# A hybrid DeltaNet / RWKV-7 layer on one core: output passes that sum in PSUM by an identity product, five input buffers, and loads placed with a lead time

## The chip, the core and the metric

The kernel runs on one core of one Trainium2 chip. A core has TensorE (PE; its weight loads are shown as PEld), VectorE (DVE), ScalarE (ACT), GpSimd (POOL) and SyncE (SP), which here issues every DMA. Each engine executes its own instructions strictly in the order in which the program lists them; semaphores hold an instruction back until its inputs are there. The metric is the device time of one launch in microseconds (us); lower is better.

## What is computed

A backbone layer with a batch of one, 512 latent tokens, a 256-token context prefix and 2048 channels. Cut to what matters:

```python
h  = rmsnorm(x)   * (1 + scale) + shift          # and hc for the context
u  = h @ w_in                                    # (512, 2048) @ (2048, 8 kinds x 8 slots x 128 and some small columns)
ya = gdn_mixer(uc, u)                            # gated DeltaNet, 8 heads of 128, both directions
yb = rwkv_mixer(uc, u)                           # RWKV-7, 16 heads of 64, both directions
x  = x + gate[:, None] * (concat([ya, yb]) @ w_out)   # the output projection, contraction over 2048 channels
return rmsnorm(x, final_norm_g)
```

Everything is fp32. A large product is made of three matmuls in the chip's fp32r format: each operand is split into a high and a low part, and high x high, high x low and low x high are summed.

## The kernel before, in words

**Slots.** The heads are worked off in eight slots: slot i holds DeltaNet head i and RWKV heads 2i and 2i+1. After a front (conditioning, norms, small projections) the context phase runs through the eight slots, then the latent phase through the eight slots again. In each slot `mixer` does: preparation (`prep_g`, `prep_r`, `prep_d`, `blocks`), `send` (a triangular matrix Z goes to DRAM as DA), `solve` (30 elimination steps on DVE, each one product solT and one update solNL; the result goes to DRAM as DD), `levels` (loads lt and Z from DD, and 96 small matmuls in the latent phase), `chain` (8 dependent steps over the chunks of 64 tokens) and `outp` (norms and gates; y is stored to the DRAM tensor yd). The chains of two slots alternate between two sets of buffers ("lanes"), so slot i+2 can only be prepared when slot i has left its lane.

**Big products.** The projections of the latent tokens (`proj`) fill PE beside the mixers until the third latent slot. The output projection follows in four *passes* (`out_pass`): pass 0 takes the y of slots 0 and 1, pass 1 slots 2 and 3, pass 2 slots 4 and 5, pass 3 slot 6; slot 7 is done at the end by `out_last`. Passes 0 to 2 are made of 16 output tiles with 12 matmuls of 128x512 each, pass 3 of 16 tiles with 6. In the trace a pass's PSUM tile is accl, its weights are wh and wl (from wr), its input is yh and yl. The running sum stays in DRAM (`rt_d`, in the trace rtd): for each tile ACT takes the PSUM result times the gate into xt, POOL adds xr (the sum so far, loaded from rtd; x itself in pass 0), and SP stores xt to rtd. Pass 3 adds rtd into the SBUF tensor rt by one DVE instruction.

**What sets the order.** The kernel is first recorded, then a list scheduler (`Rec.schedule`) plans a start for each instruction from a table of costs, and the instructions are written out in the planned order of each engine. Three of its rules matter here. An edge between instructions of different engines has a latency from `LAT`; between two of the same engine from `OWN`, and where `OWN` has no entry, the second counts as free to start as soon as the first has *started*. SP has no entry, so the load that follows a store of the same DRAM data is planned right behind it. Matmuls of jobs and passes have a `fill` flag: they are taken where PE has nothing else, or has been too idle lately. And where PE would be idle too long, the scheduler puts in *warm* matmuls (wm<-zero, 128 columns of zeros) that do nothing but keep PE active. The plan is only an order: on the chip every instruction starts when its engine reaches it and its semaphores are there.

Of the kernel before, what the change touches and what calls it, by code (L numbers as in the profile page):

```python
# [148 lines left out]
OWN = {"V": 120, "A": 148, "G": 107}  # L149
# [118 lines left out]
class Op:  # L268
    __slots__ = ("eng", "fn", "args", "kw", "npred", "succ", "ready", "dur", "tiles", "need", "prio", "idx", "src",
                 "end", "ps", "bytes", "key", "hold", "rows", "passes", "sync", "pos", "load", "fill", "bun", "cells", "cls", "lock")  # L270
# [10 lines left out]
class Rec:  # L281
    hook = None

    def __init__(self, tc, cfg):
        import concourse.bacc as bacc
        self.tc, self.nc, self.cfg = tc, tc.nc, cfg
        self.scratch = bacc.Bacc("TRN2", target_bir_lowering=False, num_devices=1)
        self.protos, self.ops, self.tiles, self.lastpool = {}, [], [], None
        self.lookidx = 0
        self.psum_last, self.shift, self.fill, self.bun, self.nbun = {}, 0, 0, None, 0  # L290
        self.engs = {"V": self.nc.vector, "A": self.nc.scalar, "G": self.nc.gpsimd, "T": self.nc.tensor, "S": self.nc.sync}
# [12 lines left out]
    def new(self, eng, fn, args, kw):  # L304
        o = Op()
        o.eng, o.fn, o.args, o.kw = eng, fn, args, kw
        o.npred, o.succ, o.ready, o.tiles, o.need, o.end, o.bytes = 0, [], 0.0, [], [], None, 0
        o.sync, o.load, o.pos, o.fill = [], 0, -1, self.fill if eng == "T" else 0
        o.idx = len(self.ops)
        o.key = o.idx + self.shift  # L310
        o.bun = self.bun if eng == "T" else None
        if o.bun:
            o.bun.ops.append(o)
        o.src = Rec.hook() if Rec.hook else None
        self.ops.append(o)
        return o
# [35 lines left out]
    def record(self, eng, fn, args, kw):  # L352
# [41 lines left out]
        for a, sync in preds.items():  # L394
            if a.eng == eng:
                lat = OWN.get(eng, -1) if sync else -1
            else:
                lat = LAT.get(a.eng + eng, 0) if sync else 0
            self.edge(a, o, lat)
# [841 lines left out]
class Kernel:  # L1241
# [51 lines left out]
    def setup(self):  # L1293
# [3 lines left out]
        self.hl = self.pool("hl", side="right")  # L1297
        self.hc = self.pool("hc", side="right")
# [60 lines left out]
    def front(self):  # L1359
# [59 lines left out]
        for kt in range(KT):  # L1419
# [12 lines left out]
            ar = fp.tile([P, 256], F32, tag="ar", bufs=2, name=self.nm("ar"))  # L1432
# [40 lines left out]
        self.ul = self.pool("ul")  # L1473
# [104 lines left out]
    def bcast_rows(self, dst, col, nj, ones, pool, psum):  # L1578
        for g in range(0, nj, 4):
            m = min(4, nj - g)  # L1580
            ps = psum(g // 4)
            for j in range(m):
                dg = pool.tile([P, P], F32, tag="dg", bufs=2, name=self.nm("dg"))
# [17 lines left out]
    def proj(self, kind, i, ctx, lat, part=None):  # L1601
# [19 lines left out]
        if lat:  # L1621
            t = self.ul.tile([P, SEQ], F32, tag="ul", bufs=2, name=self.nm(kind))
# [25 lines left out]
    def u_load(self, kind, i):  # L1648
        tag = "uz" if kind[1] == "z" else "u"
        t = self.u[(kind, i, 1)] = self.mp.tile([P, SEQ], F32, tag=tag, bufs=(3, 1)[tag == "uz"], name=self.nm(kind))  # L1650
# [88 lines left out]
    def main(self):  # L1739
# [27 lines left out]
        for i in range(NSLOT):  # L1767
# [5 lines left out]
            if i == n0:  # L1773
                self.hl.release()
# [25 lines left out]
    def passes(self, i):  # L1800
        for p in self.cfg.get("passes", {"3": [0], "5": [1], "7": [2]}).get(str(i), []):
            self.rec.shift = self.cfg.get("osh", 1000)
            self.rec.fill = self.cfg.get("ofill", 9000)
            self.out_pass(p)
            self.rec.shift = self.rec.fill = 0
# [4 lines left out]
    def y_load(self, src, eng=None):  # L1810
        self.yh, self.yl = self.y_tiles()
        for q, j in enumerate(src):
            y = self.yl[:, q].bitcast(F32)
            self.S.dma_start(y, self.y_d[j])
            self.y_split(q, y, eng)
# [5 lines left out]
    def out_pass(self, p):  # L1821
# [5 lines left out]
        for i in range(KT):  # L1827
# [4 lines left out]
            else:  # L1832
                o = 2 * (i % 2)
                if o == 0:
                    hi, lo = self.split(self.I["wout"][24 + 8 * p + i // 2].rearrange("p (k m) -> p k m", m=P), eng)
            for k in range(n):
                for m, (w, hx) in enumerate(((hi, yh), (hi, yl), (lo, yh))):
                    self.mm(ps, w[:, o + k], hx[:, k], k == 0 and m == 0, k == n - 1 and m == 2)
            g = self.dvo["gt"][:, i:i + 1]
            if p == 3:  # L1840
                r = self.rt[:, i]
                self.S.dma_start(r, self.rt_d[:, i])
                self.stt(r, ps, g, r, ALU.mult, ALU.add)
                continue
            x, r = (self.xp.tile([P, SEQ], F32, tag=t, bufs=2, name=self.nm(t)) for t in ("xr", "xt"))
            self.S.dma_start(x, self.rt_d[:, i] if p else self.I["xt"][:, i, 0:SEQ])
            self.act(r, ps, AF.Copy, scale=g)
            self.tt(r, r, x, ALU.add, self.G)
# [60 lines left out]
    def close(self):  # L1909
# [4 lines left out]
        self.ul.release()  # L1914
# [27 lines left out]
```

## Time and profile before

| | us |
|---|---|
| median of 3 runs | 2160.66 (2158.78 to 2163.45) |
| the profiled execution | 2166.2 |
| its span in the trace | 2164.4 |
| PE busy | 1966.3 (91%) |
| DVE busy | 1475.2 (68%) |
| ACT busy | 815.9 (38%) |
| POOL busy | 640.2 (30%) |

PE's busy time contains 1846 warm matmuls. It is therefore no measure of how much PE has to do; the rows below tell the warm matmuls and the passes apart. PE names in the trace go by buffer: wm, pss and br are PSUM tiles that the mixers use, accl and accc those of the big products; "wm<-zero" alone is a warm matmul.

### The profile page before, as it was taken

The numbers are of one execution on the slowest core, as the hardware profiler recorded it, in microseconds if no ns is written. First come the engines' busy times: TensorE is split into PE (matmuls) and PEld (weight loads), VectorE is DVE, ScalarE is ACT, GpSimd is POOL, SyncE is SP. The second block draws the span as 40 slices with busy tenths as digits, with TensorE's granted clock in tenths as the row PEclk, the third lists the DMA queues.
The fourth block names the chain that finished last, engine by engine and source line by source line (L and its number), as shares of the span: only waits on it lengthen the run. The fifth ranks groups of instructions, "written<-read, shape, count | busy, mean of one in ns | idle before, by whom it ended". The sixth has DMA issues, their size and how long they took to land.

```text
span 2164.4 us, 44432 instructions
## 1 busy us (share of the span) xinstructions
PE 1966.3 (91%) x16999; PEld 1542.0 (71%) x17000; DVE 1475.2 (68%) x3397; ACT 815.9 (38%) x2127; POOL 640.2 (30%) x799
## 2 busy tenths in 40 slices
PE   7999999999999999999999999978887897889877
PEld 5678887777877778776777777756665666667666
DVE  6436578675867769574765865786868577767747
ACT  4443333333242433324434434436424452435235
POOL 0003404213140421101212202235823564246226
PEclk8999999999999999999999999999979899899998
DMA  8964433333333333344541542544631544044702
GB/s 305 358 221 109 114 92 95 94 89 88 95 98 90 103 101 88 84 114 124 143 133 47 157 128 67 177 140 143 202 87 44 150 154 136 24 123 123 229 12 97
DMA packets 230517, 269.33 MB, mean 124 GB/s; under 512 B 117280, under 2 KB 130080, under 8 KB 226208
## 3 DMA queue, kind: packets, MB, share of 16 engines
q1 hardware_dynamic: 230304, 266.49, 41.8%
q8 instruction: 133, 2.18, 0.4%
q14 instruction: 80, 0.66, 0.1%
HBM read 210.50 MB, written 55.89 MB: 123 GB/s over the span
## 4 chain that ended last, share of the span: by engine, by line
PE 51%; DVE 22%; DMA 12%; issue 5%; SPq 5%; ACT 3%; POOL 3%; DVEq 0%; ACTq 0%; POOLq 0%
PE accl L705 23%; PE wm L705 8%; PE pss L705 7%; PE br L705 7%; PE accc L705 6%; DVE solNL L705 6%; SPq L705 5%; DVE solT L705 4%; DMA DD<-solNL 3%; DVE Gk L705 3%; DVE wl L705 2%; DMA DA<-Z 1%; DVE t L705 1%; DMA solNL<-DA 1%; DMA yl<-yd 1%
## 5 line engine op out<-in xcount | busy, mean ns | idle before, releaser
L705 ACT ACTIVATE wh<-wr 128x512 fp32r<-128x512 f32 x312 | 196.1, 629 | 375.5 <-PE accc L705 144.3
L705 PE MATMUL accl<-hhi,wl 128*128 128x512 f32 x768 | 317.1, 413 | 10.9 <-DVE wl L705 10.9
L705 PE MATMUL accl<-hhi,wh 128*128 128x512 f32 x768 | 314.1, 409 | 1.8 <-issue 1.8
L705 PE MATMUL accl<-hlo,wh 128*128 128x512 f32 x768 | 312.7, 407 | 0.0
L705 DVE TENSOR_TENSOR wl<-wr,wh 128x512 fp32r<-128x512 f32 x264 | 187.6, 713 | 106.9 <-ACT wh L705 102.5
L705 PE MATMUL accl<-yh,wh 128*128 128x512 f32 x480 | 199.3, 418 | 22.0 <-ACT yh L705 13.8
L705 PE MATMUL accl<-yl,wh 128*128 128x512 f32 x480 | 198.7, 414 | 0.1
L705 PE MATMUL accl<-yh,wl 128*128 128x512 f32 x480 | 197.1, 412 | 1.5 <-DVE wl L705 0.9
L705 PEld LDWEIGHTS accl<-hhi,wl 128*128 128x128 f32 x768 | 146.9, 191 | 50.9 <-DVE wl L705 13.3
L705 DVE TENSOR_TENSOR solNL<-solNL,solT 48x30 f32<-48x30 f32 (+29 forms) x480 | 175.2, 365 | 10.3
L705 DVE TENSOR_TENSOR solT<-solNL 48x30 f32<-48x30 f32 (+29 forms) x480 | 170.6, 355 | 9.0
L705 POOL TENSOR_TENSOR SRd<-Sbd,Dd 64x128 f32<-64x128 f32 x160 | 71.1, 444 | 354.2 <-DVE Sbd L705 348.1
L705 PE MATMUL wm<-zero 128*128 128x128 bf16 x1846 | 146.2, 232 | 30.3 <-DVE SG L705 15.0
L705 PEld LDWEIGHTS accl<-hhi,wh 128*128 128x128 f32 x768 | 146.9, 191 | 20.6 <-issue 4.3
L705 PEld LDWEIGHTS accl<-hlo,wh 128*128 128x128 f32 x768 | 147.0, 191 | 20.2 <-issue 3.2
L705 PEld LDWEIGHTS <-zero 128*128 128x128 bf16 x1864 | 124.4, 105 | 51.7 <-issue 46.6
L705 PE MATMUL accc<-clo,wh 128*128 128x256 f32 x512 | 149.9, 293 | 0.0
L705 PE MATMUL accc<-chi,wh 128*128 128x256 f32 x512 | 147.6, 288 | 0.0
L705 PE MATMUL accc<-chi,wl 128*128 128x256 f32 x512 | 145.9, 285 | 0.0
L705 PEld LDWEIGHTS accl<-yh,wh 128*128 128x128 f32 x480 | 90.9, 191 | 43.2 <-ACT yh L705 15.0
L705 PEld LDWEIGHTS accc<-clo,wh 128*128 128x128 f32 x512 | 97.3, 190 | 24.1 <-issue 0.9
L705 PEld LDWEIGHTS accc<-chi,wh 128*128 128x128 f32 x512 | 97.3, 190 | 21.5 <-issue 0.7
(312 smaller groups left out, 4207.8 us busy)
## 6 DMA issues: line engine op xcount, KB each, us to landing
wr<-win SPq DMA_DIRECT2D x256, 256.0 KB, 3.2
wa<-wada SPq DMA_DIRECT2D x32, 1024.0 KB, 6.0
ud<-Gk SPq DMA_DIRECT2D x72, 256.0 KB, 2.6
gw<-wada SPq DMA_DIRECT2D x64, 256.0 KB, 3.5
wr<-wout SPq DMA_DIRECT2D x64, 256.0 KB, 2.9
Rk<-ud SPq DMA_DIRECT2D x48, 256.0 KB, 3.2
rtd<-xt SPq DMA_DIRECT2D x48, 256.0 KB, 2.2
xr<-rtd SPq DMA_DIRECT2D x32, 256.0 KB, 3.0
```

The costliest lines, as they stand in the source:

```text
L705: r = getattr(self.engs[o.eng], o.fn)(*args, **kw)
```

## The change

Five edits, none of which alters what the kernel computes.

1. **The sum over passes.** Passes 0 to 2 store the bare PSUM result to rtd (no gate, no POOL add). Passes 1 to 3 load the sum so far and let PE add it: an fp32 product of the identity with the loaded tile opens the accumulation of each output tile. Pass 3 ends with the one DVE instruction that multiplies by the gate and adds x, which is now loaded into rt from the input.
2. **Five buffers** instead of three for the loaded inputs u of the latent phase (Rk, Gk, Rr, Gv, Gq, Rv). Room comes from `ul`, which now is released in the middle of the latent phase; the second part of two-part projections takes its buffer from xp instead (in the trace such tiles, and the pass's x, are called Rr).
3. **Single buffers in the front** for ar and dg.
4. **Lead times.** A DMA recorded with `dsl` set counts as landing 2500 ns later in the plan (loads of the passes) or 6000 ns later (the passes' y).
5. **SP's own dependency** gets an entry in `OWN`: a DMA that needs an earlier DMA is planned 1500 ns after that one's landing instead of right behind its issue.

```diff
-OWN = {"V": 120, "A": 148, "G": 107}
+OWN = {"V": 120, "A": 148, "G": 107, "S": 1500}
...
                 lat = LAT.get(a.eng + eng, 0) if sync else 0
+                lat += a.dsl * sync
...
-            ar = fp.tile([P, 256], F32, tag="ar", bufs=2, name=self.nm("ar"))
+            ar = fp.tile([P, 256], F32, tag="ar", bufs=1, name=self.nm("ar"))
...
-                dg = pool.tile([P, P], F32, tag="dg", bufs=2, name=self.nm("dg"))
+                dg = pool.tile([P, P], F32, tag="dg", bufs=1 + (pool.name == "fin"), name=self.nm("dg"))
...
-        t = self.u[(kind, i, 1)] = self.mp.tile([P, SEQ], F32, tag=tag, bufs=(3, 1)[tag == "uz"], name=self.nm(kind))
+        t = self.u[(kind, i, 1)] = self.mp.tile([P, SEQ], F32, tag=tag, bufs=(5, 1)[tag == "uz"], name=self.nm(kind))
...
-            t = self.ul.tile([P, SEQ], F32, tag="ul", bufs=2, name=self.nm(kind))
+            pool, tag = (self.xp, "xr") if part == 1 else (self.ul, "ul")
+            t = pool.tile([P, SEQ], F32, tag=tag, bufs=2, name=self.nm(kind))
...
             if i == n0:
+                self.ul.release()
...
+            self.rec.dsl = self.cfg.get("odsl", 2500)
             self.out_pass(p)
+            self.rec.dsl = 0
...
+            d, self.rec.dsl = self.rec.dsl, self.cfg.get("ydsl", 6000)
             self.S.dma_start(y, self.y_d[j])
+            self.rec.dsl = d
...
+            if p:
+                x = self.xp.tile([P, SEQ], F32, tag="xr", bufs=2, name=self.nm("xr"))
+                self.S.dma_start(x, self.rt_d[:, i])
+                self.mm(ps, self.cs("ident"), x, True, False)
...
             if p == 3:
                 r = self.rt[:, i]
-                self.S.dma_start(r, self.rt_d[:, i])
+                self.S.dma_start(r, self.I["xt"][:, i, 0:SEQ])
                 self.stt(r, ps, g, r, ALU.mult, ALU.add)
                 continue
-            x, r = (self.xp.tile([P, SEQ], F32, tag=t, bufs=2, name=self.nm(t)) for t in ("xr", "xt"))
-            self.S.dma_start(x, self.rt_d[:, i] if p else self.I["xt"][:, i, 0:SEQ])
-            self.act(r, ps, AF.Copy, scale=g)
-            self.tt(r, r, x, ALU.add, self.G)
+            r = self.xp.tile([P, SEQ], F32, tag="xt", bufs=2, name=self.nm("xt"))
+            self.act(r, ps, AF.Copy)
             self.S.dma_start(self.rt_d[:, i], r)
```

Since the edits change the plan's inputs, the scheduler orders every engine anew. Over the whole program the instruction counts that differ are few: 48 POOL additions go, 48 identity products (accl<-Rr,cst 128x512) come, and the warm matmuls fall from 1846 to 1349. Two places show what moved.

**PE in the chain of the last slot** (slot 7; the products with SG, Sbd and SV open a step, those with Xs and VO follow in it). Before, the gaps between the chain's matmuls hold only warm ones:

```order
L705 MATMUL wm_0_124<-zero_0_65 128x128
L705 MATMUL wm_0_124<-SG_1_9315,KQ_0_12642 128x128 x2
L705 MATMUL pss_0_125<-Sbd_1426,KR_2_12647 128x128
L705 MATMUL pss_0_125<-Sbd_1426,KR_3_12648 128x128
L705 MATMUL pss_0_125<-SV_0_12649,Z_0_12641 64x64 x4
L705 MATMUL accc_0_134<-vn_0_9322,Z_0_12641 64x128 x2
L705 LDWEIGHTS zero_0_65
L705 MATMUL wm_0_124<-zero_0_65 128x128
L705 MATMUL pss_0_125<-Xs_0_9318,Z_0_12641 64x64 x4
L705 MATMUL wm_0_124<-VO_0_12636,Z_0_12641 64x128 x2
```

After, at the same place of a step of the same chain:

```order
L707 MATMUL accl_1_145<-yh_0_77,wl_2_1441 128x512
L707 MATMUL accl_0_144<-Rr_0_12489,cst_60 128x512
L707 MATMUL accl_0_144<-yh_0_77,wh_2_1438 128x512
L707 MATMUL wm_0_129<-SG_1_9339,KQ_0_12503 128x128 x2
L707 MATMUL pss_0_130<-Sbd_1429,KR_2_12508 128x128
L707 MATMUL pss_0_130<-Sbd_1429,KR_3_12509 128x128
L707 MATMUL pss_0_130<-SV_0_12510,Z_0_12502 64x64 x4
L707 MATMUL accc_0_139<-vn_0_9346,Z_0_12502 64x128 x2
L707 MATMUL accl_0_144<-yl_0_78,wh_2_1438 128x512
L707 MATMUL accl_0_144<-yh_0_77,wl_2_1441 128x512
L707 MATMUL pss_0_130<-Xs_0_9342,Z_0_12502 64x64 x4
L707 MATMUL wm_0_129<-VO_0_12497,Z_0_12502 64x128 x2
```

Pass 2 and pass 3 reach into the last slot's chain and beyond: behind the last slot's levels stand 131 pass matmuls and 18 identity products where none stood, and 144 warm matmuls where 324 stood.

**SP between a solve's result and the loads that need it**, latent slot 4. Before, the first load from DD stands directly behind the store:

```order
L705 DMA DD_0_119<-solNL_1424 96x2x1024
L705 DMA lt_0_9312<-DD_0_119 32x12x32
L705 DMA yd_111<-ot_1_9326 128x512
L705 DMA Gz_0_9292<-ud_110 128x512
L705 DMA Z_0_9337<-DD_0_119 32x12x32 x2
```

After, other transfers stand in between, among them a store of the pass's result (rtd<-xt), which waits for ACT, and loads of the sum so far (Rr<-rtd), which wait until PE has used their buffer:

```order
L707 DMA DD_0_124<-solNL_1427 96x2x1024
L707 DMA rtd_117<-xt_1_12492 128x512
L707 DMA Rr_1_12490<-rtd_117 128x512
L707 DMA wr_2_1435<-wout 128x512
L707 DMA Rk_0_9311<-ud_115 128x512
L707 DMA rtd_117<-xt_0_12491 128x512
L707 DMA Rr_0_12489<-rtd_117 128x512
L707 DMA lt_0_9336<-DD_0_124 32x12x32
```

In the program before, no DMA stands between store and first load at any of the 16 solves; after, one to eight do at each of them.

## Rows read from the trace of the kernel before

**Rows 1.** Stages of the latent phase by window, each from one slot's levels to the next.

```profile
core 0: us, PE busy (x) PEld busy (x) DVE busy (x) ACT busy (x) POOL busy (x), PEclk, DMA share, GB/s
...
1456.91:1591.32 134.41, 116.03 (x1175) 87.36 (x1174) 95.67 (x194) 58.81 (x159) 82.94 (x86) 0.95 0.52 158
1591.32:1683.61 92.29, 72.34 (x973) 56.81 (x972) 67.24 (x181) 35.17 (x114) 27.18 (x44) 0.88 0.24 66
1683.61:1823.84 140.23, 121.37 (x1264) 93.04 (x1262) 99.74 (x205) 58.77 (x162) 81.84 (x88) 0.93 0.49 145
1823.84:1918.68 94.84, 73.06 (x972) 56.98 (x971) 67.37 (x181) 35.24 (x114) 27.03 (x44) 0.87 0.23 65
1918.68:2044.85 126.17, 117.08 (x1039) 87.11 (x1037) 92.66 (x192) 50.55 (x122) 61.19 (x68) 0.95 0.59 178
2044.85:2164.39 119.54, 88.86 (x1145) 77.43 (x1144) 65.03 (x146) 49.45 (x131) 46.25 (x57) 0.88 0.18 56
```

**Rows 2.** The same windows, PE instructions on yh alone (two of each pass's three matmuls).

```profile
core 0: us, PE busy (x), PEclk, DMA share, GB/s
...
1591.32:1683.61 92.29, 2.77 (x8) 0.88 0.24 66
1683.61:1823.84 140.23, 45.02 (x120) 0.93 0.49 145
...
1918.68:2044.85 126.17, 64.19 (x180) 0.95 0.59 178
```

**Rows 3.** Two of the windows, PE instructions on zero (warm) alone.

```profile
1591.32:1683.61 92.29, 18.91 (x220) 0.88 0.24 66
1683.61:1823.84 140.23, 21.90 (x307) 0.93 0.49 145
```

**Rows 4.** Chain of waits: start us, length us, what; a run of 39 accl.

```profile
1994.49 9.11 PE accl L705 x39
```

**Rows 5.** Timeline of PE: start us, length us, instructions; warm, and fp32 of 512 columns.

```profile
1077.81 1.02 PE L705 MATMUL br<-t,cst 128*128 128x512 f32 x2
1078.67 0.60 PE L705 MATMUL br<-cst,t 128*128 128x128 f32 x4
...
2113.14 3.73 PE L705 MATMUL wm<-zero 128*128 128x128 bf16 x33
2116.63 0.56 PE L705 MATMUL accl<-yh,fh 128*128 128x256 f32 x1
```

**Rows 6.** Waits of PE: us in total, times, longest us.

```profile
PE wm L705 <- DMA lt<-DD: 29.0, 26, 2.6
...
PE accl L705 <- ACT yh L705: 14.6, 9, 3.2
...
PE accl L705 <- DVE wl L705: 11.8, 8, 3.2
```

**Rows 7.** Waits of SP's queue.

```profile
SPq L705 <- POOL xt L705: 80.7, 35, 6.7
...
SPq L705 <- DMA DD<-solNL: 60.0, 16, 4.7
```

**Rows 8.** Tile xt: instructions, duration ns min/median/max.

```profile
L705 POOL TENSOR_TENSOR xt<-xt,xr x48: 1261/1288/1751, 1482.9 to 2015.8; 128x512 f32<-128x512 f32 x48
```

**Rows 9.** Timeline of DVE and POOL in slot 5's solve.

```profile
1790.49 1.42 POOL L705 TENSOR_TENSOR xt<-xt,xr 128x512 f32<-128x512 f32 x1
1790.72 1.34 DVE L705 TENSOR_TENSOR KR<-t,t 128x126 f32<-128x126 f32 x1
1791.88 1.30 POOL L705 TENSOR_TENSOR wl<-wr,wh 128x512 fp32r<-128x512 f32 x1
1791.98 1.46 DVE L705 TENSOR_TENSOR solNL<-solNL,solT 96x240 f32<-96x240 f32 x1
1793.37 0.27 DVE L705 TENSOR_TENSOR KR<-t,t 128x126 f32<-128x126 f32 x1
1793.57 0.39 DVE L705 TENSOR_TENSOR solT<-solNL 96x238 f32<-96x238 f32 x1
```

**Rows 10.** Chain of waits in the front, the dg products.

```profile
32.76 2.13 PE br L705 x8
36.42 0.64 PE br L705 x4
```

**Rows 11.** Tile rt, DVE instructions, duration ns min/median/max.

```profile
L705 DVE SCALAR_TENSOR_TENSOR rt<-accl,dv,rt x32: 466/610/751, 2023.0 to 2144.9; 128x512 f32<-128x512 f32 x16, 128x256 f32<-128x256 f32 x16
```

More of the change, by code (lines that the diff above doesn't have):

```diff
@@ L269 @@
     __slots__ = ("eng", "fn", "args", "kw", "npred", "succ", "ready", "dur", "tiles", "need", "prio", "idx", "src",
-                 "end", "ps", "bytes", "key", "hold", "rows", "passes", "sync", "pos", "load", "fill", "bun", "cells", "cls", "lock")
+                 "end", "ps", "bytes", "key", "hold", "rows", "passes", "sync", "pos", "load", "fill", "bun", "cells", "cls", "lock", "dsl")
     def clone(self):
@@ L290, in __init__ @@
         self.psum_last, self.shift, self.fill, self.bun, self.nbun = {}, 0, 0, None, 0
+        self.dsl = 0
         self.engs = {"V": self.nc.vector, "A": self.nc.scalar, "G": self.nc.gpsimd, "T": self.nc.tensor, "S": self.nc.sync}
@@ L308, in new @@
         o.sync, o.load, o.pos, o.fill = [], 0, -1, self.fill if eng == "T" else 0
-        o.idx = len(self.ops)
+        o.idx, o.dsl = len(self.ops), self.dsl if eng == "S" else 0
         o.key = o.idx + self.shift
@@ L1297, in setup @@
         self.hl = self.pool("hl", side="right")
+        self.ul = self.pool("ul", side="right")
         self.hc = self.pool("hc", side="right")
@@ L1472, in front @@
         self.wp = self.pool("wp")
-        self.ul = self.pool("ul")
         self.upA = self.pool("upA")
@@ L1835, in out_pass @@
                     hi, lo = self.split(self.I["wout"][24 + 8 * p + i // 2].rearrange("p (k m) -> p k m", m=P), eng)
+            if p:
+                x = self.xp.tile([P, SEQ], F32, tag="xr", bufs=2, name=self.nm("xr"))
+                self.S.dma_start(x, self.rt_d[:, i])
+                self.mm(ps, self.cs("ident"), x, True, False)
             for k in range(n):
                 for m, (w, hx) in enumerate(((hi, yh), (hi, yl), (lo, yh))):
-                    self.mm(ps, w[:, o + k], hx[:, k], k == 0 and m == 0, k == n - 1 and m == 2)
+                    self.mm(ps, w[:, o + k], hx[:, k], not p and k == 0 and m == 0, k == n - 1 and m == 2)
             g = self.dvo["gt"][:, i:i + 1]
@@ L1913, in close @@
         self.mp.release()
-        self.ul.release()
         self.wp.release()
```

## The prediction

> **What bounds the kernel now.** I read the stages first, because the page's 91% for PE mixes three things. Up to the third latent slot PE works off the projections and is full. From there on the kernel goes by slots, and their stages alternate: 134.4, 92.3, 140.2, 94.8 and 126.2 us, then 119.5 us to the end [rows 1]. The passes explain the alternation. The stage that begins with slot 3's levels has 8 matmuls on yh, the next has 120 [rows 2]; two of three pass matmuls read yh, so these are 12 and 180 pass matmuls. A pass matmul takes 9.11 / 39 = 0.234 us when PE is fed [rows 4], so 168 more of them are 39.3 us. The second stage also has 307 - 220 = 87 more warm matmuls [rows 3]. It is 47.9 us longer. If the passes are charged in full, (47.9 - 39.3) / 87 = 0.10 us is left for each warm matmul, and warm ones in a row are (2116.63 - 2113.14) / 33 = 0.106 us apart [rows 5]. The two stages thus differ by just what PE was given in addition: the passes are not hidden beside the mixers but add to the stages, and so does the filler. PE's list of work, filler included, sets the pace of this part, through an order fixed beforehand. Around it lie waits that the order did not foresee. PE stands 29.0 us before levels whose lt is still landing, 14.6 us before passes whose yh is late, and 11.8 us before big products whose wl is late [rows 6].
>
> **The change part by part.**
>
> *Identity products.* 48 of them come. An fp32 product with 512 columns goes as two rows of PE; the pair begins at 1077.81 and the next product at 1078.67 [rows 5], so 0.86 us each, 41.3 us together. The lower bound is zero, if each falls into a gap that would have been idle; the upper is 48 x 1.02 = 49 us, the length of the pair. I take 41.3, since the stages above charge PE's work in full.
>
> *Warm matmuls.* 497 fewer. The bounds come from their own busy time, 21.90 / 307 = 0.07 us, and their spacing, 0.106 us [rows 3, 5]: -35 to -53 us. Below that the end is zero, if they stood only where PE would have waited anyway. I take 0.10, what the two stages leave: -49.7 us. With the identity products PE's list is 8.4 us shorter. Where the passes stand does not enter this term: their number is unchanged.
>
> *SP's own dependency.* Before, SP goes from the store of DD straight to the load of lt and stands there for 60.0 us in 16 solves, 3.8 us each [rows 7], with every later load behind it in its queue. After, one to eight other transfers are issued in that time, and the plan puts the levels where lt can have landed, so that PE does other work instead of standing. The 29.0 us of PE [rows 6] are worth between zero (PE then waits at the next thing) and all. I take half, -14 us. The weights that were queued behind the blocked load come earlier, too; of the 11.8 us before wl I take -5, between 0 and 11.8.
>
> *Lead time of y.* The 14.6 us in nine waits for yh are 1.6 us each. A lead of 6 us in the plan covers them. At most -14.6, at least zero; I take -9, since some of these waits stand before matmuls that the next dependency would have held.
>
> *The POOL additions.* 48 x 1.288 = 62 us of POOL go [rows 8]. POOL is not the bottleneck, but it disturbs DVE while DVE solves. A step of the solve with 240 elements takes 1.46 us beside POOL's wl, the next with 238 takes 0.39; DVE's 126-element product takes 1.34 us beside POOL's xt, and 0.27 alone [rows 9]. So one addition in the way costs up to about 1.07 us of DVE: 48 x 1.07 = 51 us is the upper end, zero the lower (DVE not on the path, or held by wl's splits instead, which stay on POOL). I take a quarter, -12 us, since passes and solves share only the ends of three stages, and half of POOL's work in a pass stays. The Trainium skill, "SBUF — State Buffer", section "SBUF: two separate sides", says that a DVE instruction with two SBUF inputs and a GpSimd one exclude each other for the whole instruction, whichever starts first. The stretched steps agree with it (0.39 us against 1.46). By this rule each addition could hold DVE for its full 1.288 us and the term would be -62 us at most.
>
> *ACT and the stores.* ACT's copy drops its scale and stays one instruction per tile; the store to rtd no longer waits for POOL, on which SP's queue now stands 80.7 us in 35 waits [rows 7]. I cost the relief at nothing, because other loads of the same passes stand right behind it; it is cover for SP's new transfers.
>
> *Five input buffers, ul.* Priced at nothing. Earlier loads let a slot be prepared earlier, but the slot before the last must still leave its lane; what the buffers help beyond that shows as the shorter PE list, counted above.
>
> *Front.* With one dg buffer, DVE's scaling and PE's product take turns. The products now take 2.13 and 0.64 us [rows 10]; three more turns of about a microsecond are +3 us at most on this chain, if nothing hides them, and zero if PE's later projections do. I take +3, with ar's single buffer in it.
>
> *The tail.* Part of pass 3 now stands among the last slot's final products. Its 16 DVE instructions on rt of 0.6 to 0.75 us [rows 11] ran before the last chain; in the order about half come after it, where DVE is also needed for the end: 8 x 0.75 = +6 us, lower end zero.
>
> *Sum.* -8.4 - 14 - 5 - 9 - 12 + 3 + 6 = -39.4 us. Against the profiled execution's 2166.2 us that is 2126.8. That execution lies 5.5 us above the median of the runs, so the forecast is **2121 us**.
>
> **Rivals.**
>
> *A. The passes become hidden.* The stages without passes have room: 92.3 - 72.3 = 20 us idle and 18.9 us warm in one of them, and 30.7 us idle in the last stage [rows 1, 3]. The new order does spread passes over these, the last chain included. If half of what the three long stages have over 93.6 us (the mean of the two short ones) goes, that is half of 40.8 + 46.6 + 32.6 = 60 us in place of 8.4: -60 - 31 = -91, so 2070 us. Against it: passes in a chain's gaps delay the next step, because PE is in order.
>
> *B. The filler was no time.* If warm matmuls filled only waits of the mixers, dropping them gives nothing and the identity products come on top: +41.3 - 31 = +10.3, so 2171 us. The comparison of the two stages speaks against it.
>
> *C. PE stands before the identity product.* Slower. Before, it was POOL that waited for xr; now it is PE, with the chain's matmuls queued behind it and ACT and DVE waiting for those. The load is issued by SP in order, behind stores that wait for ACT, and only once the buffer's last user on PE is done. At the 1.6 us that each late yh cost, 48 waits are +78 us, so 2199 us. It decides from 39.4 / 48 = 0.82 us per product on; the 2.5 us of lead speak against it.
>
> *D. The clock.* The stages with few passes have a granted clock of 0.88 and 0.87 in spite of over 200 warm matmuls; those with passes 0.93 to 0.95 [rows 1]. With 497 fewer warm ones, the three long stages might fall to 0.875 of full speed: 354.5 us of PE x (0.944 / 0.875 - 1) = +28 us, so 2149 us. "TensorE: Matmul & The Clock Gate" of the Trainium skill, "What's actually happening", says that the slow clock is the default and activity lifts it, which would count against a shorter filler. Where passes take the filler's place, activity stays, which the higher clock of the pass stages bears out.
>
> *E. The solve's loads are late.* What SP does between DD and lt now contains stores that wait for ACT and loads that wait for PE. If three of these hold SP by the 2.3 us that a store waited on average (80.7 / 35) [rows 7], six latent solves lose 6 x 6.9 = 41 us, and the 14 us of lt are not won: 2121 + 55 = 2176 us.
>
> *F. Nothing.* Gains and new waits cancel: 2160 us.
>
> **How the numbers follow.** Forecast 0.48 (on its own 2095 to 2145: the terms' unknown ends of half their size), A 0.20, B 0.09, C 0.07, D 0.07, E 0.05, F 0.04. Faster by over 0.2% (4.3 us, about what a measurement can tell here) are the forecast, A and D: 0.75, and a little of F, so 0.76. Within 0.2% 0.06 from F and the edges of B and D; slower 0.18. The range runs from A's 2070 to E's 2176, rounded outwards at the lower end for passes hidden by more than half: 2066 to 2176; C lies outside.
>
> **What would show it.** Right: waits of PE for lt and for yh at less than half, no wait of accl for Rr among PE's long ones, solve steps above 1 us rarer, and the alternation of long and short stages weaker. Wrong: PE waiting for Rr's landing; SP waiting for ACT xt between DD and lt; the stage after the last levels longer than 119.5 us by more than the earlier ones are shorter; the front longer by more than the 3 us allowed for it.

## The result, and the profile after

The changed kernel takes **2077.48 us** (median of 4 runs, 2072.82 to 2083.05); the kernel before, beside it, 2162.05 us (4 runs, 2158.78 to 2168.2). The ratio is 0.9607, 95% interval [0.9572, 0.9641]: 85 us faster. The forecast was 41 us faster; direction and range held, the size was half of what came, and the time lies 7 us above rival A's 2070.

The profiled execution has a span of 2071.0 us with 1935.6 us of PE busy, so PE stands 135.4 us, where it stood 2164.4 - 1966.3 = 198.1. Stages by window, the columns as in [rows 1]; the first line is the context phase, from its first to its last slot's levels, the next runs from there to the levels of latent slot 2, the others from slot to slot to the end:

```profile
322.31:942.37 620.06, 608.52 (x4752) 492.38 (x4752) 471.17 (x1168) 215.83 (x564) 158.28 (x190) 1.00 0.36 99
942.37:1455.48 513.11, 493.23 (x3671) 375.44 (x3670) 350.55 (x732) 222.61 (x568) 134.65 (x170) 0.99 0.50 140
...
1455.48:1529.74 74.26, 57.56 (x837) 44.76 (x836) 55.04 (x160) 27.80 (x95) 17.00 (x33) 0.89 0.22 60
1529.74:1653.04 123.30, 103.35 (x1180) 77.09 (x1178) 97.57 (x224) 50.10 (x152) 53.59 (x71) 0.96 0.38 105
1653.04:1749.50 96.46, 88.15 (x924) 62.67 (x923) 72.31 (x177) 43.13 (x127) 36.07 (x49) 0.96 0.53 153
1749.50:1850.29 100.79, 82.14 (x1061) 61.71 (x1059) 85.68 (x206) 43.90 (x138) 40.92 (x60) 0.98 0.32 81
1850.29:1929.09 78.80, 75.86 (x825) 53.43 (x824) 56.98 (x154) 35.50 (x95) 28.95 (x43) 1.00 0.47 134
1929.09:2071.00 141.91, 120.38 (x1132) 92.13 (x1131) 83.25 (x172) 56.52 (x144) 48.52 (x58) 0.92 0.43 141
```

The first two of these stretches in the kernel before:

```profile
315.78:966.65 650.87, 619.64 (x4764) 500.12 (x4764) 472.07 (x1167) 215.31 (x564) 162.30 (x194) 0.98 0.36 95
966.65:1456.91 490.26, 458.38 (x3487) 347.64 (x3486) 332.54 (x730) 197.72 (x518) 97.76 (x145) 0.98 0.44 124
```

So 30.8 us of the 93.4 us between the two spans lie in the context phase, where there are no output passes and one warm matmul; the prediction did not look there. The front, ahead of it, is 6.5 us longer. In the latent part, the stages of 134, 92, 140, 95 and 126 us have become 74, 123, 96, 101 and 79, and the last stage grew by 22 us, 92 us less in the six together; but the stretch before them is 23 us longer (513.1 against 490.3), so the whole part is 69 us shorter. PE's instructions on yh (two of each pass's three matmuls) go with this; columns as in [rows 2]:

```profile
1455.48:1529.74 74.26, 0.00 (x0) 0.89 0.22 60
1529.74:1653.04 123.30, 22.44 (x53) 0.96 0.38 105
1653.04:1749.50 96.46, 30.59 (x75) 0.96 0.53 153
1749.50:1850.29 100.79, 11.92 (x30) 0.98 0.32 81
1850.29:1929.09 78.80, 29.84 (x76) 1.00 0.47 134
1929.09:2071.00 141.91, 62.46 (x216) 0.92 0.43 141
```

Before, the first five stages held 132, 8, 120, 8 and 180 instructions on yh. Now pass 0 stands wholly in the longer stretch ahead of them (192 on yh from slot 1's to slot 2's levels, where 64 were), the first stage holds none, and passes 1 to 3 are spread over the other five. (The count in the last stage includes records of the final products that read yh, before and after alike.)

Waits of PE, columns as in [rows 6]:

```profile
PE wm L707 <- DVE SG L707: 13.5, 19, 1.9
PE pss L707 <- DVE ot L707: 10.7, 8, 2.2
...
PE accl L707 <- DVE wl L707: 4.6, 5, 3.0
PE accl L707 <- DVE Rr L707: 4.4, 2, 3.1
...
PE accl L707 <- ACT yh L707: 0.7, 1, 0.7
```

The 29.0 us before lt are gone altogether, yh fell from 14.6 to 0.7 us, wl from 11.8 to 4.6. Waits of SP's queue, as in [rows 7]:

```profile
SPq L707 <- ACT xt L707: 43.8, 19, 8.9
...
SPq L707 <- DMA DD<-solNL: 11.9, 10, 3.9
```

SP's 60.0 us behind DD are 11.9. It does wait for ACT's xt, as rival E feared, but PE's lt did not come late for it. Warm matmuls of the kernel before and of the changed one (count, busy us, mean ns, idle before them and what ended it):

```profile
L705 PE MATMUL wm<-zero 128*128 128x128 bf16 x1846 | 146.2, 232 | 30.3 <-DVE SG L705 15.0 <-ACT vn L705 6.9 <-ACT vt L705 6.5
```

```profile
L707 PE MATMUL wm<-zero 128*128 128x128 bf16 x1349 | 108.1, 234 | 22.6 <-ACT vn L707 9.5 <-DVE SG L707 7.8 <-ACT vt L707 3.3
```

The identity products, two records each, and how little PE stood before them (1.7 us in all):

```profile
L707 PE MATMUL accl<-Rr,cst 128*128 128x512 f32 x96 | 50.7, 610 | 1.7 <-ACT xt L707 1.7
```

These lines also split the gain by PE. PE stands 62.7 us less (198.1 to 135.4). Its warm matmuls take 38.1 us less and the identity products 50.7 us more. All its other work, the same matmuls before and after, takes 43.3 us less (1966.3 - 146.2 = 1820.1 before, 1935.6 - 108.1 - 50.7 = 1776.8 after). The mean granted clock rose from 0.955 to 0.977 of 2.4 GHz, and 1820.1 x 0.955 / 0.977 = 1779 us, so the higher clock would account for nearly all of the 43 us. This is an estimate: no run changes the clock alone.

### The profile page after: what moved, and what is told of

It reads as the page before. It is cut to its first block, busy times and chain, and to the rows that moved or that the text cites. A ratio compares the mean times of both kernels' runs of the same rounds, so it can differ in the third digit from the quotient of the medians.

```text
span 2071.0 us, 43566 instructions
## 1 busy us (share of the span) xinstructions
PE 1935.6 (93%) x16598; PEld 1501.4 (72%) x16599; DVE 1455.5 (70%) x3397; ACT 811.7 (39%) x2127; POOL 575.9 (28%) x751
## 5 line engine op out<-in xcount | busy, mean ns | idle before, releaser
L707 PE MATMUL accl<-yh,wh 128*128 128x512 f32 x480 | 210.1, 440 | 7.5 <-DVE Rr L707 4.4
L707 PE MATMUL accl<-yh,wl 128*128 128x512 f32 x480 | 198.1, 413 | 1.9 <-POOL wl L707 1.9
L707 DVE TENSOR_TENSOR solNL<-solNL,solT 48x30 f32<-48x30 f32 (+29 forms) x480 | 168.8, 352 | 10.8
L707 POOL TENSOR_TENSOR SRd<-Sbd,Dd 64x128 f32<-64x128 f32 x160 | 65.6, 410 | 349.8 <-DVE Sbd L707 343.5
L707 PE MATMUL wm<-zero 128*128 128x128 bf16 x1349 | 108.1, 234 | 22.6 <-ACT vn L707 9.5
L707 PEld LDWEIGHTS <-zero 128*128 128x128 bf16 x1367 | 94.1, 106 | 43.3 <-issue 39.3
```

Source lines behind the costliest of these rows:

```text
L707: r = getattr(self.engs[o.eng], o.fn)(*args, **kw)
```

## The experiments

Each kernel was timed beside the kernel before on the same chip; the ratio is to that. The kernel before took 2152 to 2167 us beside different ones, so kernels are compared by their ratios, and a point (0.01) is some 21.6 us; a difference of medians can be off by several us. Most expectations number their theories and say what each holds; the questions in order were: which of the five edits carry the gain, what the S entry really buys, and what the POOL additions really cost.

| kernel | median us | ratio to before, 95% interval |
|---|---|---|
| after | 2077.5 | 0.9607 [0.9572, 0.9641] |
| own_only | 2103.8 | 0.9725 [0.9679, 0.9771] |
| own_undone | 2117.7 | 0.9765 [0.9730, 0.9801] |
| lead_undone | 2070.1 | 0.9549 [0.9517, 0.9580] |
| bufs3 | 2083.4 | 0.9619 [0.9589, 0.9648] |
| pe_view | 2182.5 | 1.0101 [1.0042, 1.0159] |
| sp_order | 2155.2 | 0.9986 [0.9960, 1.0012] |
| own_ident | 2068.9 | 0.9588 [0.9542, 0.9633] |
| pool_sum | 2110.0 | 0.9782 [0.9738, 0.9827] |
| own_noprod | 2072.5 | 0.9611 [0.9557, 0.9665] |
| ident_pool | 2132.3 | 0.9867 [0.9809, 0.9926] |
| ident_only | 2109.6 | 0.9773 [0.9724, 0.9822] |
| dve_split | 2039.4 | 0.9443 [0.9399, 0.9486] |
| ident_memset | 2073.7 | 0.9602 [0.9555, 0.9649] |
| pe_ident | 2138.6 | 0.9890 [0.9835, 0.9944] |
| sp_ident | 2117.8 | 0.9803 [0.9747, 0.9858] |
| best5 | 2041.5 | 0.9452 [0.9407, 0.9497] |
| sp_held | 2039.6 | 0.9458 [0.9416, 0.9500] |
| pool_blind | 2074.0 | 0.9621 [0.9585, 0.9656] |

### Which edits carry the gain

**own_only**: the kernel before with edit 5 alone.

```diff
-OWN = {"V": 120, "A": 148, "G": 107}
+OWN = {"V": 120, "A": 148, "G": 107, "S": 1500}
```

> The kernel before with edit 5 alone (OWN gets S: 1500); a change of order only. Theory 1 (waits the plan did not foresee): PE's 29 us before lt go, SP's blocked loads come earlier, and the context phase alone shrinks by 25 to 30 us as it did in the changed kernel; with the later slots about -45 us: 2117 us, and no wait of PE for lt left. Theory 2 (the passes became hidden through identity sum and five buffers; the context's gain comes from elsewhere): 2150 to 2160 us.

2103.8 us, 2.75% (59 us of 2160) from one number in a table. Context phase, and PE on yh in the stages from latent slot 3's to slot 7's levels, of this kernel:

```profile
317.87:939.24 621.37, 608.70 (x4754) 492.50 (x4753) 471.36 (x1168) 216.13 (x564) 156.82 (x190) 1.00 0.37 99
```

```profile
1553.29:1686.55 133.26, 39.39 (x115) 1.00 0.48 140
1686.55:1778.63 92.08, 6.97 (x17) 0.98 0.37 103
1778.63:1875.67 97.04, 11.07 (x28) 0.95 0.32 81
1875.67:1988.22 112.55, 49.05 (x139) 0.97 0.60 188
```

The context phase is as short as in the changed kernel. The time is 13 us below theory 1's 2117. This kernel has 1994 warm matmuls, 148 *more* than before, and is 2.75% faster; a price of 0.10 us on each warm matmul would have made it 15 us slower by that term.

**own_undone**: the changed kernel without that entry.

> The changed kernel without edit 5 (no S entry in OWN). Theory 1: the 29 us of PE before lt come back and the context phase is again near 650 us: about 2077 + 45 = 2122 us. Theory 2: the passes stay hidden, at most the lt waits of the last slots come back: 2080 to 2092 us.

0.9765 against 0.9607. PE's wait for lt is back in full, and the context phase takes 975.32 - 315.85 = 659 us again:

```profile
PE wm L707 <- DMA lt<-DD: 29.0, 30, 1.8
```

**lead_undone**: the changed kernel with both lead times at 0.

```diff
-            self.rec.dsl = self.cfg.get("odsl", 2500)
+            self.rec.dsl = self.cfg.get("odsl", 0)
-            d, self.rec.dsl = self.rec.dsl, self.cfg.get("ydsl", 6000)
+            d, self.rec.dsl = self.rec.dsl, self.cfg.get("ydsl", 0)
```

> The changed kernel with both lead times of edit 4 at zero. Theory 1: the waits for yh come back (14.6 us before) and PE waits before identity products for Rr as well, 1 us each in 48: +15 to +60 us, 2092 to 2137 us. Theory 2: loads have their cover in the spread passes: within 8 us of 2077.

2070.1 us: the leads gain nothing. If anything they lose a little (0.9549 [0.9517, 0.9580] without, 0.9607 [0.9572, 0.9641] with; the intervals just touch). Even without them PE waits for yh 3.5 us only.

**bufs3**: the changed kernel with three input buffers.

```diff
-    bufs=(5, 1)[tag == "uz"]
+    bufs=(3, 1)[tag == "uz"]
```

> The changed kernel with three input buffers again (edit 2 without its buffers). Theory 1: the buffers are worth nothing by themselves: within 10 us of 2077. Theory 2: without them a slot's preparation stands behind the slot before it, the passes bunch in every second stage again: 2110 to 2130 us, with the stages of the later slots alternating as before.

2083.4 us; the ratios differ by 0.12 points (some 3 us) and the intervals overlap. What the buffers are worth can't be told from nothing.

**own_ident**: the kernel before with the S entry and the identity sum alone, three buffers and no leads.

> The kernel before with edits 5 and 1 (S entry and the sum by the identity product), three buffers, no lead times. Theory 3 (the rest of the gain, 26 us from the S entry alone at 2104 to the full change, is POOL's additions gone): 2075 to 2085 us. Theory 4 (the rest comes from the earlier loads of five buffers, the identity product costs PE 41 us and returns as much): 2095 to 2110 us.

0.9588 against 0.9607: these two edits are the whole gain.

**ident_only**: the identity sum alone.

> The kernel before with edit 1 alone. If the two edits that matter add up (S entry -63, identity sum -35): 2165 - 35 = 2130 us. If the identity sum needs the realistic landing times: 2150 to 2165 us. The changed kernel without the S entry took 2118, which speaks for the sum or a little better.

0.9773. Singly the edits give 2.75% and 2.27%, together 4.12%; they overlap by 0.9 points. The waits for lt stay under the identity sum alone (33.1 us in 29). The last lump of passes is spread: from slot 2's levels on, the stages hold 139, 20, 108, 36 and 70 instructions on yh. The first two lumps stay nearly as they were, and yet their stages take 117.4 and 111.2 us instead of 134.4 and 140.2. So with the identity sum a lump also costs less where it stands, and the gain is not only that passes are spread. At 2109.6 us the kernel is faster than the figures of all its expectations.

**pool_sum**: the changed kernel with ACT's gate and POOL's addition back in place of the identity products.

> The changed kernel with the sum again by ACT's scale and POOL's addition (edit 1 undone, the rest kept). Theory 3: 2098 to 2108 us, DVE's solve steps stretched again beside xt. Theory 4: 2070 to 2085 us, since PE is spared 41 us.

0.9782 against 0.9607: in the changed kernel the identity sum is worth 1.75 points, or 38 us of 2160.

### What the S entry buys

The entry does two things in the plan: it gives the levels on PE a due time when lt can have landed, and it lets SP issue other transfers in between. Two pairs of kernels separate the halves: *pe_view* and *pe_ident* count the loads of solve and levels as landing 5 us later and leave SP's place alone; *sp_order* and *sp_ident* have the S entry and count the same loads as landing 5 us earlier, so that SP's order changes and PE's due times stay as they were. The first of each pair starts from the kernel before, the second from ident_only.

```diff
+        k.rec.dsl = 5000        # pe_view, pe_ident; -5000 and the S entry in sp_order, sp_ident
         ... the loads solNL<-DA, and lt, Z<-DD
+        k.rec.dsl = 0
```

> The kernel before, whose plan counts the loads of solve and levels (solNL<-DA, lt and Z<-DD) as landing 5 us later; SP has no entry, so the first load still stands right behind the store in SP's queue and SP stands there as before (60 us at DD). Theory P (PE's order, made for too early a landing, was the loss): nearly all of edit 5's gain: 2100 to 2120 us, PE no longer waiting for lt. Theory Q (SP's blocked queue, weights and next loads late behind it, was the loss): 2150 to 2165 us.

> The reverse: S: 1500 in OWN, so that SP issues other transfers between store and load, but the same loads counted as landing 5 us earlier, so that PE and DVE are ordered about as before. Theory P: little, 2145 to 2165 us, PE's wait for lt still 20 us or more. Theory Q: most of the gain, 2105 to 2120 us.

> ident_only with the loads of solve and levels counted as landing 5 us later, no S entry. In the context phase pe_view won 22 us, sp_order 9, both together 30. If the halves add up where POOL is relieved: 2110 - 25 = 2080 to 2090 us. If PE's view needs SP unblocked in the latent phase, as without the identity sum: 2100 to 2130 us.

> ident_only with the S entry, but the same loads counted as landing 5 us earlier. If the halves add up: 2110 - 12 = 2095 to 2102 us. If SP's order alone were the gain: 2070 to 2080 us. If it is worth nothing alone: 2105 to 2115 us.

Over the whole program neither half gains. PE's view alone is 1.0% *slower* than before, and with the identity sum 1.2 points behind ident_only; SP's order alone is level (0.9986), or 0.3 points behind (intervals overlap). In the context phase both do gain: it takes 628.6 us in pe_view and 641.7 in sp_order, 22 and 9 us less than before, nearly the 29.5 us of own_only together. What pe_view wins there it loses elsewhere: its front is 9.7 us longer and all that follows the context phase 37 us.

```profile
325.51:954.11 628.60, 607.71 (x4725) 491.20 (x4724) 472.03 (x1161) 213.29 (x555) 166.59 (x190) 0.99 0.35 97
```

Waits of PE in pe_view and its SP line:

```profile
PE accl L707 <- ACT xt L707: 16.4, 12, 5.3
...
PE accl L707 <- ACT yh L707: 12.6, 5, 8.1
PE br L707 <- ACT KQ L707: 11.7, 7, 7.6
```

```profile
SPq L707 <- DMA DD<-solNL: 62.2, 16, 5.3
```

The lt wait is gone (1.1 us), but SP stands as long as ever behind DD while the plan believes that its later transfers are already under way. Other things come late instead, yh by up to 8.1 us at a time; that they come late by SP's queue is a reading of these waits, not a run of its own. In sp_order the wait for lt stays:

```profile
PE wm L707 <- DMA lt<-DD: 25.6, 32, 1.6
```

**sp_held** asks whether the blocked queue itself is the price. It is ident_only; in addition the plan holds SP's whole queue until the store has landed, as the chip does. lt stays right behind DD (no DMA stands between them at any of the 16 solves), and SP stays as blocked as before. The rule holds for every DMA that needs an earlier DMA, so also for the passes' loads from rtd and yd.

```diff
+            if e == "S" and o.spred:                     # spred: earlier DMAs that this DMA needs
+                s = max(s, max(a.end for a in o.spred) + 1500)
```

> The kernel before with the sum by the identity product; in addition the plan holds SP until the DMA that its next load waits for has ended and 1.5 us more have passed, so that PE's due times carry the landing and SP's order keeps each lt load right behind its DD store, as the chip's blocked queue does. SP is thus as blocked in the plan as on the chip. Theory 3 (what counts is that plan and chip agree on SP): the landing is covered by passes, the other loads are not late, and the time is 2069 to 2085, like own_ident (2068.9), with under 3 us of lt waits in the 'PE waits' view. Theory 9 (the blocked queue is itself the price, agreement only shows it in the plan): the lt waits go but loads behind are late in the plan too, and the time stays at 2100 to 2118, near ident_only (2109.6). A time over 2125, as pe_ident (2138.6), would say that both are wrong.

2039.6 us, 0.9458 [0.9416, 0.9500]: better than own_ident's 0.9588 [0.9542, 0.9633] and than the changed kernel. Its SP queue, PE's wait for lt, and the context phase:

```profile
SPq L708 <- DMA DD<-solNL: 65.4, 16, 5.7
```

```profile
PE wm L708 <- DMA lt<-DD: 1.3, 2, 0.9
```

```profile
318.29:924.69 606.40, 602.48 (x4742) 490.17 (x4741) 472.82 (x1162) 213.73 (x560) 158.03 (x190) 1.00 0.38 100
```

SP stands 65.4 us, more than before, in all 16 solves, and the ratio fell from ident_only's 0.9773 to 0.9458. So the blocked queue was not the price; the price was a plan that didn't know of it. pe_ident is the contrast: SP as blocked (60.2 us) and PE's wait for lt gone too (1.3 us), but its plan counts only the loads as landing later and not what stands behind them in SP's queue, and its ratio is 0.9890, slower than both of its theories. The theory expected 2069 to 2085 us and 2039.6 came. Holding the queue is thus better here than issuing past it; why by that much (14 us of it in the context phase, 606.4 us against own_ident's 620.6) was not separated.

### What the POOL additions cost

**own_noprod**: own_ident with the 48 identity products left out, so that the partial sums are not added.

```diff
-                self.mm(ps, self.cs("ident"), x, True, False)
```

> own_ident without its 48 identity products (the loads of the sum stay; the passes' partial sums are therefore not added up). As the prediction priced them, 0.86 us each on PE's list: 2069 - 41 = 2028 us. If they stand where PE had nothing else to do (theory 5: PE's list is elastic, only its dependent part counts): within 12 us of 2069.

0.9611 [0.9557, 0.9665] against 0.9588 [0.9542, 0.9633]: no gain. But PE's list is not shorter by the products alone, since the scheduler put 323 warm matmuls more in. own_ident's and own_noprod's:

```profile
L705 PE MATMUL wm<-zero 128*128 128x128 bf16 x1350 | 108.5, 231 | 19.7 <-ACT vn L705 6.8 <-DVE SG L705 4.7 <-ACT vt L705 3.5
```

```profile
L705 PE MATMUL wm<-zero 128*128 128x128 bf16 x1673 | 131.9, 230 | 26.3 <-DVE SG L705 8.7 <-ACT vn L705 7.1 <-ACT vt L705 6.0
```

So the run shows that the products cost no more than the filler that takes their place. By the prediction's own prices the list would be 41.3 - 32.3 = 9 us shorter, which this measurement can't tell from nothing. That both stand where PE had nothing else to do fits own_only, where more filler went with less time; no run left the filler out.

**ident_pool**: lead_undone (with four buffers for room) and, for each tile, a POOL addition on data that nobody reads.

```diff
             self.S.dma_start(self.rt_d[:, i], r)
+            j = self.xp.tile([P, SEQ], F32, tag="xj", bufs=1, name=self.nm("xj"))
+            self.tt(j, r, r, ALU.add, self.G)
```

> The changed kernel without lead times and with four input buffers, and with 48 POOL additions of the removed kind put back on dead data: each reads xt and writes a spare tile; nobody waits for the result. If POOL's work itself costs (theory 3: DVE's solve steps are held while POOL adds): 2070 + 25 to 35 = 2095 to 2105 us. If the loss lay in the way over POOL (PSUM to ACT to POOL to store, with SP waiting for POOL; theory 6): 2065 to 2080 us.

2132.3 us, 0.9867: 3.2 points or 69 us slower than lead_undone (62 by the medians), though nothing waits for these additions' results, and more than either theory held. Passes 1 and 2 lie in lumps again (PE on yh, stages from slot 2's levels to the end):

```profile
1477.34:1551.81 74.47, 0.00 (x0) 0.84 0.16 37
1551.81:1712.86 161.05, 49.88 (x128) 0.94 0.47 133
1712.86:1805.46 92.60, 0.00 (x0) 0.80 0.24 61
1805.46:1942.93 137.47, 41.25 (x103) 0.95 0.41 119
1942.93:2017.65 74.72, 10.41 (x25) 0.97 0.36 102
2017.65:2139.60 121.95, 52.41 (x192) 0.92 0.40 130
```

**ident_memset**: the same with three POOL clears in place of the addition, to load POOL without the exclusion.

> As ident_pool, but in place of each addition on dead data POOL clears the spare tile three times: POOL is occupied for about as long (3 x 0.46 us by the plan's figure), but reads nothing. Theory 7 (the cost is DVE being held by a POOL instruction that reads SBUF): near 2070, at most 2085 us. Theory 8 (POOL's occupation itself costs, since other POOL work of the mixers stands behind it): 2110 to 2135 us as with the additions.

2073.7 us, but it decides nothing: the 144 clears depend on nothing and all ran from 1326.2 to 1491.7 us, beside pass 0 and ahead of passes 1 to 3:

```profile
L707 POOL MEMSET xj<- x144: 517/525/1190, 1326.2 to 1491.7; 128x512 f32 x144
```

**pool_blind** mends this. It is ident_pool, with the additions on the chip as they were; only the plan counts them as work that shuts VectorE out no more than a clear does, and as 1395 ns long instead of 1225.

```diff
+            if args[0].t.key == "xj":
+                o.lock, o.dur = 1, 1395
```

> ident_pool (48 POOL additions on data that nobody reads, beside the identity products; 2132.3) with one change in the plan alone: it counts these additions as work that does not shut VectorE out, so the passes are spread over the last stages as without them. The additions still run on the chip beside the passes. Theory 7 (the price of POOL's additions is paid on the chip, by VectorE's instructions being held up beside them): 2110 to 2135, with stretched VectorE steps in the stages that hold passes. Theory 8 (the price is in the order that the plan makes when it believes that they shut VectorE out: passes bunched in a few stages): 2070 to 2090, near lead_undone (2070.1).

2074.0 us, where ident_pool took 2132.3 (ratios 0.9621 and 0.9867). The same additions run beside the passes:

```profile
L707 POOL TENSOR_TENSOR xj<-xt x48: 1029/1046/2385, 1399.0 to 1981.3; 128x512 f32<-128x512 f32 x48
```

```profile
L709 POOL TENSOR_TENSOR xj<-xt x48: 1032/1046/1505, 1394.3 to 1952.9; 128x512 f32<-128x512 f32 x48
```

but the passes are spread (PE on yh, same stages):

```profile
1450.37:1542.38 92.01, 2.23 (x7) 0.93 0.30 84
1542.38:1653.03 110.65, 19.30 (x48) 0.92 0.34 92
1653.03:1763.13 110.10, 34.72 (x84) 0.98 0.54 157
1763.13:1858.71 95.58, 7.29 (x20) 0.93 0.28 72
1858.71:1948.97 90.26, 41.33 (x105) 1.00 0.49 146
1948.97:2074.40 125.43, 51.91 (x192) 0.94 0.44 146
```

and there are 1330 warm matmuls where ident_pool has 1677. VectorE is disturbed more, not less: summed over its instructions that run beside a POOL one, the time above the lower quartile of the same form is some 127 us in pool_blind, 117 in ident_pool and 97 in lead_undone. So the additions do stretch VectorE's steps on the chip, but the difference to ident_pool, 2.5 points or 53 us, is the plan's, which counts a POOL addition as shutting VectorE out. That this works by keeping passes and solves apart is read from the stages; the order inside the stages changed too.

What is left for the chip is small and not well known. Against lead_undone it is 4 us by the medians (2074.0 and 2070.1) and 0.72 points, 16 us, by the ratios (0.9621 [0.9585, 0.9656] and 0.9549 [0.9517, 0.9580]), and lead_undone has five buffers. Against ident_memset, which has four as well, it is 0.2 points with overlapping intervals.

### A version that beats both

**dve_split** is own_ident with the splits of the passes' weights and y on VectorE too; **best5** is that with the five buffers and their room, without leads.

```diff
-        eng = self.G if p < 3 else None
+        eng = None
```

> own_ident with the passes' splits (wl and yl) on DVE as well, so that POOL has no part in the passes at all. By theory 3 the splits on POOL hold DVE for some 25 us, while on DVE they cost 48 x 0.69 + 12 x 0.69 = 41 us of work: 2060 to 2085 us; if DVE has room between the steps of chain and solve, the lower end.

> dve_split's splits on DVE in the changed kernel without lead times (five buffers). If the buffers are worth nothing: 2039 within 8 us. If they help once POOL is out of the passes: 2020 to 2030 us.

dve_split takes 2039.4 us, 0.9443, below its expectation's 2060 to 2085: 1.6 points, some 35 us, below the changed kernel; the buffers add nothing (best5, 0.9452). Against own_ident POOL's busy time falls from 579.8 to 494.6 us, PE's from 1938.7 to 1913.0. It has 1135 warm matmuls; only sp_ident has fewer, 1094, at 2117.8 us, so the number of warm matmuls does not rank the kernels. Whether this gain, too, is the plan's rather than the chip's was not tried, nor was dve_split together with sp_held's queue.

## Why the prediction was right or wrong, step by step

**"PE's list of work, filler included, sets the pace of this part" - wrong, and the root of the rest.** Two stages of one plan fitted this account to a microsecond, but they were two stages of one order, and the account was its property. 148 warm matmuls more go with 59 us less in own_only. 48 products of 0.86 us less, with 323 warm matmuls in their place, change nothing measurable in own_noprod. So the identity products' +41.3 us came out at nothing beyond the filler they replace, and the warm matmuls' -49.7 us is no term at all: the filler's number follows from the order, and does not price it. What changed the time in place of the list is what the plan knew: SP's landing (own_only, 59 us) and POOL's additions (pool_blind against ident_pool, 53 us).

**"POOL is not the bottleneck ... I take a quarter, -12 us" - wrong in size and mechanism.** Identity, warm and POOL terms gave -8.4 - 12 = -20.4 us together. Measured were 2.27% alone (49 us) and 1.75 points in the changed kernel (38 us). The contention I priced is real but costs between nothing measurable and 16 us (pool_blind). What I didn't look for is that the scheduler has the same exclusion among its rules (`blocked` in `Rec.schedule`), so that an addition on POOL also changes where passes and solves are planned. The Trainium skill's rule ("SBUF — State Buffer", "SBUF: two separate sides"), that a VectorE instruction with two SBUF inputs and a GpSimd one that reads SBUF shut each other out, put the term at -62 us at most, an estimate with the 1.288 us of [rows 8]. ident_pool lost about as much, 62 us by the medians and 69 by the ratios, but pool_blind shows that the agreement is by chance: the stretching that the rule describes is there, most of that cost is not.

**"Where the passes stand does not enter this term" - wrong.** The passes were moved, the alternation of long and short stages is weaker, and the latent part is 69 us shorter; how much of this is the passes' place alone no run separates, since ident_only's lumps cost less in place, too. Rival A, at 2070 us and with a chance of 0.20, said that passes which fall into the room of the short stages are hidden. What it had against it, that passes in a chain's gaps delay the chain, came in part: the last stage is 22 us longer with 131 pass matmuls and 18 identity products more, which at 0.234 and 0.86 us are 46 us (28 us after 180 warm ones fewer at 0.10). So they are at best half hidden there. That A's time is so near is partly luck: it keeps the forecast's 31 us of other terms, of which the waits, the lead and POOL's part were mis-sized or wrong, and has nothing of the context phase's 30.8 us.

**"The 29.0 us of PE are worth between zero and all. I take half, -14 us", and wl's -5 - wrong by its bounds.** The entry measured 59 us alone and 1.85 points (40 us) beside the identity sum, more than both waits in full (40.8 us) in the one case and as much in the other. The bound was wrong because the 29 us are only where a false due time shows first. pe_view takes nearly all of them away and is slower; sp_held leaves SP's 60 us in place and is one of the three fastest kernels, which their intervals do not tell apart. The prediction read the wait and not the model error behind it. Half of the entry's 59 us, 29.5, and a third of the whole gain, 30.8, lie in the context phase, where PE waited only 8.3 us for lt and 10.9 for wl before.

**y's lead, -9 us - wrong.** The waits for yh went (14.6 to 0.7 us), but they go to 7.2 us with the S entry alone, and to 3.5 in the changed kernel without the leads; taking the leads out loses nothing.

**Five buffers 0 - right** within what the runs can tell. **Front +3** - right in sign, by another cause: the front is 6.5 us longer after (322.31 against 315.78), more than the 3 us allowed for, but 315.85 in own_undone, which has dg and ar single. So it needs the S entry, though the entry alone brings only 2.1 us (own_only, 317.87); what brings the rest beside it stays open. **Tail +6** was not measured by itself; it lies within the last stage's +22.

**Rivals.** B's time did not come, but its premise, that the filler was no time, is what own_only speaks for; what B had wrong is that the identity products come on top. C fell: PE stands before the identity products 1.7 us in all, and the 4.4 us in two waits for Rr stand before another form, accl<-yh, at 1360 and 1376 us, ahead of the first load of the sum, and end with a DVE instruction, not with a load. D fell, and the clock worked the other way: the mean granted clock rose, 0.955 to 0.977 of 2.4 GHz, with 497 warm matmuls fewer, which by the estimate above goes with some 40 us of PE's time. Of the five stages from slot 2's to slot 7's levels, only the one without passes is below 0.96; the last stage has 0.92. E fell: SP waits for ACT xt 43.8 us, PE not at all for lt.

## What to carry to other kernels

Where a planner sets the order, look first for what its cost table believes falsely, above all an in-order queue that stands longer on the chip than in the plan: the visible wait is then neither the price nor an upper bound of it, and a repair must tell the truth to both sides, the instruction that waits and those queued behind it (here either half alone gained only in the context phase). Don't price filler or gap work from the stages of one order; leave it out in one run and see. And before a resource conflict is blamed on the chip, run the same work with the planner blind to it.

## What was not expected of the hardware

- 48 fp32 identity products with 512 columns (0.61 us a record, two records each) cost nothing measurable on a PE that is 93 to 94% busy, against a kernel with 323 warm matmuls in their place.
- POOL's addition of a tile to itself took 1.05 us at the median, the one of two tiles 1.29 us [rows 8].
- A load that waits in SP's queue for a store's landing stands 3.8 to 4.1 us on average (60.0 / 16 and 65.4 / 16), and the kernel in which the plan holds the queue for it (sp_held) is among the three fastest.
- With less waiting the granted clock of the context phase rose from 0.98 to 1.00, with one warm matmul in it before and after; PE's busy time there fell by 11 us for nearly the same number of matmuls (4764 and 4752 records).
